# First modulation in two column halves, the first two projection rows in two sets of feature blocks, and the last FFN's sums one pair later

## The chip, the core and the metric

The program runs on one core of a Trainium2 chip. The metric is the time of one execution on the device in microseconds (us); lower is better. The engines are TensorE (PE: matrix multiplies and transposes into PSUM; PEld: its weight loads), VectorE (DVE), ScalarE (ACT), GpSimd (POOL) and SyncE (SP). Here POOL and SP mostly issue DMA transfers, each from its own queue; the transfers of all queues share the core's 16 DMA engines.

## The reference, cut to what matters

Two layers of a diffusion backbone over 1024 latent tokens and 256 context tokens, width D = 1024. Each layer is a mixer and a SwiGLU FFN, each behind a modulated RMS norm. The modulation comes from a conditioning vector, one for the latents and one for the context:

```python
def ada_mod(cond, w, b):
    m = (jax.nn.silu(cond) @ w + b)[..., None, :]
    return jnp.split(m, 6, axis=-1)

def modulate(h, shift, scale):
    return h * (1.0 + scale) + shift
...
        sh1, sc1, g1, sh2, sc2, g2 = ada_mod(c, ada_w[i], ada_b[i])
        u_lat = modulate(rms_norm(h_lat, norm1_g[i]), sh1, sc1)
...
            csh1, csc1, cg1, csh2, csc2, cg2 = ada_mod(c_ctx, ada_w[i], ada_b[i])
            u_ctx = modulate(rms_norm(h_ctx, norm1_g[i]), csh1, csc1)
        if even:
            y_lat = mixer_ab(u_lat, *ab)      # begins with p = u @ w_in, w_in of 1024 x 2048
```

The last FFN is `(silu(u @ w_gate) * (u @ w_up)) @ w_down`, done with Strassen's and Winograd's scheme of seven products on 2 x 2 blocks, which needs sums of blocks of each operand, `w_down` among them.

## The kernel before

Activations lie with features on partitions: u is eight feature blocks of 128 (`KB` = 8), each over three pieces of tokens: pc 0 and pc 1 are 512 latents each, pc 2 the 256 context tokens (`PCS` = (2, 0, 1)). A float32 product is made of three multiplies of rounded parts: each operand is split into hi (`split`: ACT copies with rounding, line 350) and lo (DVE subtracts, line 352), and hi*hi, hi*lo, lo*hi are summed in PSUM by `mm` (line 346).

The head of the program does the following. `filter_mlp` runs a small two-layer MLP with sines (its tail, from line 773, splits the result for the Hyena filters). `ada_first` computes shift and scale of the first norm for both conditions: `ada_pair((1, 0), ...)` loads sixteen tiles `ada_k` of 128 x 1024 (`s<-in_ada_k`, scale and shift for each of eight blocks of the input) through POOL's queue, multiplies them by the two condition columns in four groups of 32 output rows (line 521), copies the rows out, turns them by four transposes (line 536) and adds bias and gain on DVE (lines 543 and 545). `first_norm` loads x and ctx as ten tiles of 128 tokens (`x_row`; tokens 8 and 9 are the context's tiles), squares and scales them by token (lines 698 to 709), and then, for each piece and feature block, transposes (line 727), applies scale and shift while leaving PSUM (DVE line 732, ACT line 734), and splits into u's hi and lo. `in_proj` multiplies output block by output block of w_in ("row" below) against all of u. Its first two rows are done together, three multiplies each per feature block and piece, while `first_norm` is advanced one block at a time by `next(norm)`; the results are copied out at line 1121. The later rows run with other work (filters, spectra, Fourier front) filled in.

A tile scheduler sets the order on each engine from the program and its own estimate of times, within what the data allow; `follow(x)` asks that an instruction be placed behind x. DMA issues are in the order of their queue, POOL's by `ldr`, SP's by `ld`. Pools have a fixed number of buffers: `s4` 21 tiles of 128 x 1024, `ws` 4, `wh` and `wl` 2 each, PSUM six banks `ps` and two `pq`.

In the last FFN (`ffn` with l = 1) eleven pairs of hidden blocks are worked off one after the other; in pair i the helper `sums(k)` (lines 1995 to 2008) loads four quarters of w_down, makes four sums on DVE (2003 to 2006) and stores them for the later `down`; pair i takes k = 2i-2 and 2i-1.

Of the kernel before, what the change touches and what calls it, by code (L numbers as in the profile page):

```python
# [18 lines left out]
P = 128  # L19
D = 1024  # L20
# [238 lines left out]
class Builder:  # L259
# [230 lines left out]
    def ada_first(self):  # L490

        nc, a = self.nc, self.a
        cond = self.C(46)
        nc.gpsimd.memset(cond[:, 16:], 0.0)
        self.ld(cond[:, :16], a["cond"])
        nc.scalar.activation(cond[:, :16], cond[:, :16], AF.Silu)
        self.cond32 = cond
        yield
        yield from self.ada_pair((1, 0), self.S4, self.ldr)

    def ada_pair(self, ms, tile, load):
# [10 lines left out]

        first = ms == (1, 0)
        ps = self.PP()
        ready = fetch(0)
        for kb in range(KB):
# [8 lines left out]
            yield  # L525
        if first:
            self.ada_mm = last
# [4 lines left out]
        if first:  # L532
            self.pk = (self.pk + 1) % self.banks
        for k in range(4):
# [3 lines left out]
        for c in (1, 0):  # L538
            t = self.ada[(0, c)]
            for i, m in enumerate(ms):  # L540
                sl = slice(m * 8, m * 8 + 8)
                two = lambda x: x.rearrange("p (j k) -> p j k", j=2)
                nc.vector.tensor_tensor(two(t[:, sl]), view[:, 2 * i:2 * i + 2, :, c], two(self.adab[:, sl]), ADD)
                if m == 1:
                    nc.vector.scalar_tensor_tensor(t[:, sl], t[:, sl], 1.0, self.gs[:, 0:8], op0=ADD, op1=MUL)
        yield
# [127 lines left out]
    def first_norm(self, u):  # L674
# [5 lines left out]
        for i in groups[0]:  # L680
            rows[i] = self.S4()
            self.ld(rows[i], a["x_row"][i])
        yield
        for i in groups[1]:
# [6 lines left out]
        sq = self.C(10)  # L691

        def scaled(order, cols):
            for k, i in enumerate(order):
                t = self.T(mybir.dt.bfloat16, 1024)
                if k % 2:
                    with self.follow(self.sin):
                        self.sq_act = nc.scalar.activation(t, rows[i], AF.Square, accum_out=sq[:, i:i + 1]).ins
                else:
                    with self.follow(self.clamp):  # L700
                        self.sq_dve = V.tensor_tensor_reduce(t, rows[i], rows[i], 1.0, 0.0, MUL, ADD, sq[:, i:i + 1]).ins
            for c in cols:
                nc.scalar.activation(sq[:, c], sq[:, c], AF.Sqrt, scale=1.0 / D, bias=self.eps)
                V.reciprocal(sq[:, c], sq[:, c])
            for k, i in enumerate(order):
                if k % 2:
                    nc.scalar.mul(rows[i], rows[i], sq[:, i:i + 1])
                else:
                    V.tensor_scalar(rows[i], rows[i], sq[:, i:i + 1], None, op0=MUL)

        scaled(groups[0], (slice(8, 10), slice(0, 4)))
        yield
        for pc in PCS:
            w = WID[pc]
            n = w // P
            if pc == 0:
                scaled(groups[1], (slice(4, 8),))
            u.t.update(self.new_act(pcs=(2,)).t if pc == 2 else {})
            for b in range(KB):
                c0 = b % 2 * w if pc == 2 else 0  # L720
                if c0 == 0:
                    ps = self.PS()
                if pc < 2:
                    u.t.update(self.new_act(pcs=(pc,), blocks=(b,)).t)
                for j in range(n):
                    with self.follow(self.ada_mm):
                        nc.tensor.transpose(ps[:, c0 + j * P:c0 + j * P + P],
                                            rows[OFF.get(pc, LAT) // P + j][:, b * P:b * P + P], self.ident)
                sh, sc = self.ada_col(0, pc, 0, b), self.ada_col(0, pc, 1, b)
                t = self.T()  # L730
                if pc == 2 or b % 2:
                    V.tensor_scalar(t[:, :w], ps[:, c0:c0 + w], sc, sh, op0=MUL, op1=ADD)
                else:
                    nc.scalar.activation(t, ps, AF.Identity, scale=sc, bias=sh)
                self.split(t[:, :w], u.ap(0, b, pc), u.ap(1, b, pc))
                yield

    def filter_mlp(self):
# [12 lines left out]
        for layer, w in enumerate((w1, w2)):  # L751
# [14 lines left out]
            if layer == 0:  # L766
                yield
        self.tap("mlp", x)
# [315 lines left out]

    def in_proj(self, u, norm, fill, four, conv):
        nc, a = self.nc, self.a
# [39 lines left out]
        with self.follow(self.sq_act), self.follow(self.sq_dve):  # L1126
            pairs = [self.weights(a["w_in"][nb]) for nb in (0, 1)]
        p01 = [{}, {}]
        for _ in range(4):
            next(norm)  # L1130
        for pc in PCS:
            accs = [self.PS(), self.PS()]
            for kb in range(KB):
                next(norm, None)
                for r, (wh, wl) in enumerate(pairs):
                    for w, part in ((wh, 0), (wh, 1), (wl, 0)):
                        self.mm(accs[r][:, :WID[pc]], w[:, kb * P:kb * P + P], u.ap(part, kb, pc),
                                kb == 0 and w is wh and part == 0, kb == KB - 1 and w is wl)
            for r in (0, 1):
                p01[r][pc] = kept(r, pc, accs[r])  # L1140
        next(front)
# [846 lines left out]
    def ffn(self, l, u, h, hs, second, after, keep=None, begun={}, early=()):  # L1988
# [59 lines left out]
        for i in range(NFB // 2):  # L2048
# [494 lines left out]
    def run(self):  # L2543
# [23 lines left out]
        next(mlp)  # L2567
        drain(mlp)
        drain(ada1)
        next(ng)  # L2570

# [26 lines left out]
        def conv():  # L2598
# [6 lines left out]
        fc, cc = four(), conv()  # L2605
        self.in_proj(u, ng, ((long, (1, 2, 4, 5, 5, 5, 5, 5, 6, 0)), (filt, (0,) * 9 + (3, 3, 3, 3, 2)),
                             (ada, (0,) * 5 + (1,) * 9)), fc, cc)
# [248 lines left out]
def host_layout(i):  # L2856
# [76 lines left out]
```

## Time and profile before

| | us |
|---|---|
| median of 3 runs (lowest, highest) | 2841.94 (2839.5, 2843.06) |
| profiled execution, its span | 2836.49, 2834.7 |
| TensorE busy over the span | 2756.6 |
| TensorE busy from 0 to 42.4 us, of 42.4 | 22.25 |
| TensorE busy from 42.4 to 81 us, of 38.6 | 36.42 |
| TensorE busy from 2200 to 2560 us, of 360 | 356.03 |

Rows of the timeline begin with the start and the duration, then engine, line, operation, and the tiles written and read by name (`s` is any tile of the s pools, `c` a constant); a bracket gives idle time of that engine just before and what ended it. Rows of groups end with busy time, mean ns of one, and idle time before. In rows of stretches each engine has its busy time and the number of instructions, then come the granted TensorE clock, the busy share of the DMA engines and GB/s. The profiled execution was shorter than all three timed runs, so a sum of its durations has to be set against its own time.

### The profile page before, as it was taken

What the parts mean: (1) busy time and instruction counts of PE and PEld (TensorE: products, weight loads), DVE (VectorE), ACT (ScalarE), POOL (GpSimd) and SP (SyncE); (2) the same over time, 40 slices, a digit from 0 to 9 for tenths busy, and PEclk for the clock granted to TensorE, in tenths of its full rate; (3) what the DMA queues carried; (4) which work ended last, traced back from release to release, by engine and by line L of the source; (5) the groups of instructions that cost most, each with busy time, mean ns of one, the idle gap of its engine ahead of it and who ended that gap; (6) DMA issues with size and microseconds to landing.
All of it is one profiled execution on the core that took longest, in us unless ns stands there. A gap on an engine that the chain in (4) does not pass through costs nothing. (4 is left out here: it accounts for less than half of the span.)

```text
span 2834.7 us, 43636 instructions
## 1 busy us (share of the span) xinstructions
PE 2756.6 (97%) x15610; PEld 2310.1 (81%) x15610; DVE 2042.6 (72%) x3531; ACT 1321.8 (47%) x2271; POOL 552.4 (19%) x896
## 2 busy tenths in 40 slices
PE   6999999999999999999999999999999999999998
PEld 4876778788898888888889888888887788888887
DVE  6777678768877888876777437778868977664555
ACT  5433336443654333343455337878755533333434
POOL 2220335331011222222020002332221122112000
PEclk9999999999999999999999999999999999999999
DMA  7366535665665656658884435877955366435763
GB/s 270 121 193 210 157 93 192 209 220 184 213 207 195 212 198 207 219 204 321 305 306 152 134 115 145 204 199 200 257 192 205 131 240 228 141 104 174 235 193 134
DMA packets 295862, 554.20 MB, mean 196 GB/s; under 512 B 81872, under 2 KB 128658, under 8 KB 295646
## 3 DMA queue, kind: packets, MB, share of 16 engines
q1 hardware_dynamic: 225662, 348.47, 39.6%
q0 software_dynamic: 62784, 189.84, 19.1%
q10 hardware_dynamic: 7200, 13.11, 1.4%
q8 instruction: 123, 2.02, 0.3%
q14 instruction: 93, 0.76, 0.1%
HBM read 405.01 MB, written 118.76 MB: 185 GB/s over the span
## 5 line engine op out<-in xcount | busy, mean ns | idle before, releaser
L1943 PE MATMUL ps<-s,s 128*128 128x512 f32 x2012 | 498.4, 391 | 3.3 <-DVE s L1834 1.7
L1943 PEld LDWEIGHTS ps<-s,s 128*128 128x128 f32 x2012 | 379.2, 189 | 83.9 <-DVE s L1834 2.6
L346 PE MATMUL ps<-s,wh 128*128 128x256 f32 (+1 forms) x1776 | 401.6, 330 | 8.6 <-ACT wh L350 3.8
L346 PEld LDWEIGHTS ps<-s,wh 128*128 128x128 f32 x1776 | 294.2, 189 | 44.2 <-ACT wh L350 5.2
L346 PE MATMUL ps<-s,wl 128*128 128x256 f32 (+1 forms) x888 | 268.1, 328 | 1.5 <-DVE wl L352 1.5
L350 ACT CAST s<-s 128x1024 fp32r<-128x1024 f32 (+2 forms) x196 | 174.9, 921 | 199.6 <-DMA s<-d 178.7
L2120 PE MATMUL ps<-s,s 128*128 128x512 f32 (+1 forms) x1000 | 259.6, 383 | 3.3 <-DVE s L352 3.2
L346 PE MATMUL pq<-s,wh 128*128 128x512 f32 (+1 forms) x848 | 259.7, 388 | 0.8 <-DVE s L2360 0.5
L352 DVE TENSOR_TENSOR wl<-ws,wh 128x1024 fp32r<-128x1024 f32 (+1 forms) x141 | 167.8, 1190 | 121.0 <-ACT wh L350 114.9
L350 ACT CAST wh<-ws 128x1024 fp32r<-128x1024 f32 (+1 forms) x141 | 144.7, 1026 | 211.4 <-PE ps L346 93.2
L352 DVE TENSOR_TENSOR s<-s,s 128x1024 fp32r<-128x1024 f32 (+2 forms) x174 | 193.5, 1143 | 58.1 <-ACT s L350 56.2
L346 PE MATMUL ps<-s,s 128*128 128x65 f16 (+4 forms) x2736 | 224.8, 234 | 2.6 <-DVE s L2479 0.8
L2120 PEld LDWEIGHTS ps<-s,s 128*128 128x128 f32 x1000 | 184.6, 188 | 41.0 <-DVE s L352 4.5
L350 ACT CAST s<-t 128x512 fp32r<-128x512 f32 (+2 forms) x234 | 131.5, 581 | 172.9 <-PE ps L1943 71.8
L352 DVE TENSOR_TENSOR s<-t,s 128x512 fp32r<-128x512 f32 (+2 forms) x234 | 148.1, 647 | 74.7 <-ACT s L350 54.0
L1943 PE MATMUL ps<-s,wh 128*128 128x512 f32 x624 | 194.8, 390 | 0.0
L337 POOL DMA_DIRECT2D d<-s x202 | 110.0, 546 | 379.1 <-DVE s L1750 90.5
L346 PEld LDWEIGHTS ps<-s,wl 128*128 128x128 f32 x888 | 164.5, 189 | 19.3 <-DVE wl L352 2.1
L346 PEld LDWEIGHTS pq<-s,wh 128*128 128x128 f32 x848 | 150.2, 189 | 23.0 <-DVE c L871 0.8
L346 PE MATMUL pq<-s,wl 128*128 128x512 f32 (+1 forms) x424 | 161.5, 381 | 0.7 <-DVE wl L352 0.7
L2120 PE MATMUL ps<-s 128*128 128x512 f32 (+1 forms) x500 | 150.7, 385 | 0.0
L346 PEld LDWEIGHTS ps<-s,s 128*128 128x128 f32 (+1 forms) x816 | 126.2, 191 | 20.2 <-issue 2.0
(489 smaller groups left out, 5460.3 us busy)
## 6 DMA issues: line engine op xcount, KB each, us to landing
s<-d SPq DMA_DIRECT2D x282, 256.0 KB, 4.1
d<-s POOLq DMA_DIRECT2D x186, 256.0 KB, 3.7
s<-in_down SPq DMA_DIRECT2D x150, 256.0 KB, 4.6
s<-in_ada_w POOLq DMA_DIRECT2D x64, 512.0 KB, 5.0
ws<-in_up SPq DMA_DIRECT2D x44, 512.0 KB, 3.8
d<-g POOLq DMA_DIRECT2D x86, 256.0 KB, 3.1
ws<-in_gate SPq DMA_DIRECT2D x42, 512.0 KB, 5.3
d<-tk POOLq DMA_DIRECT2D x66, 256.0 KB, 4.0
```

Of the source, the lines that this page charges most:

```text
L337: self.last_ldr = self.nc.gpsimd.dma_start(out, in_).ins
L346: self.last_mm = self.nc.tensor.matmul(o, l, r, start=st, stop=sp).ins
L350: self.last_hi = nc.scalar.copy(hi, src).ins
L352: self.last_lo = eng.tensor_tensor(lo, src, hi.bitcast(F32), SUB).ins
L1943: nc.tensor.matmul(ps, x[:, sl], y, start=first and j == 0 and x is wh and y is xh, stop=j == 3 and x is wl, skip_group_check=True)
L2120: m = nc.tensor.matmul(acc[j][:, c0:c1], x[:, sl], y[:, xs], start=first and k == 0, stop=last and k == 2, skip_group_check=True)
```

## The change

1. The weights of the first modulation are laid out anew (`ada_h`): half j holds the columns 512j to 512j+511 of scale and shift, that is, what feature blocks 4j to 4j+3 need, in eight tiles. `ada_half(0)` runs before the projection; `ada_half(1)` is loaded behind it and multiplied tile by tile inside the first two rows.
2. The two rows run in four steps (`STEPS`): context blocks 0 to 3, first latents (pc 0) blocks 0 to 7, context blocks 4 to 7, second latents (pc 1). The sums of all pieces stay in PSUM until their step is done.
3. The two rows' weights are loaded on POOL's queue between the halves, each in two column pieces, and split in two pieces. The squares and scalings of the rows of x are spread over the steps, and the MLP's tail is moved to the eighteenth of the 24 block steps.
4. In the last FFN pair i takes the sums k = 2i-4 and 2i-3.

```diff
+STEPS = ((2, range(4)), (0, range(KB)), (2, range(4, KB)), (1, range(KB)))
...
-        yield from self.ada_pair((1, 0), self.S4, self.ldr)
+        yield from self.ada_half(0)
+
+    def ada_half(self, j):
...
+        for kb in range(KB):
+            ws.append(self.S4())
+            self.ldr(ws[-1], a["ada_h"][j, kb])
+        yield
+        ps = self.PP()
+        for kb in range(KB):
+            with self.follow(self.last_mm if j else None):
+                for g in range(4):
+                    self.ada_mm = nc.tensor.matmul(ps[32 * g:32 * g + 32, :256], cond[:, 2 * kb:2 * kb + 32],
+                                                   ws[kb][:, g * 256:(g + 1) * 256], start=kb == 0, stop=kb == KB - 1,
+                                                   tile_position=(0, 32 * g), skip_group_check=True).ins
+            yield
+        row = self.G()
+        nc.vector.tensor_copy(row[:, :256], ps[:, :256])
+        col = self.PP()
+        last = self.ada_mm
+        for k in (0, 1):
+            with self.follow(last):
+                self.col_tr = nc.tensor.transpose(col[:, k * P:(k + 1) * P], row[:, k * P:(k + 1) * P], self.ident).ins
...
     def first_norm(self, u):
...
+        for i in (8, 9, 0, 1):
+            square(i, self.sin1, self.clamp if i == 0 else self.clamp1)
+        root(slice(8, 10), self.sin)
+        for i in (8, 9):
+            scale(i)
+        for i in (2, 3):
+            square(i, self.sc_act, self.clamp)
+        yield
...
-        for pc in PCS:
+        first = self.ada_mm
+        for pc, kbs in STEPS:
...
+            if (pc, kbs[0]) == (0, 0):
+                with self.follow(self.last_hi), self.follow(self.last_lo):
+                    for i in groups[0][2:]:
+                        scale(i)
...
+                if (pc, b) == (0, 5):
+                    for i in groups[1][:2]:
+                        square(i, self.last_hi, self.last_lo)
...
     def in_proj(self, u, norm, half, mlp, first_w, fill, four, conv):
...
+        def first_split(c, act, dve):
+            for t, (hi, lo) in zip(first_w, pairs):
+                with self.follow(act), self.follow(dve):
+                    self.split(t[:, c], hi[:, c], lo[:, c])
...
+        for pc, kbs in STEPS:
+            if kbs[0] == 0:
+                sums[pc] = [self.PQ() if pc == 2 else self.PP() for _ in (0, 1)]
+            for kb in kbs:
...
+                        with self.follow(self.col_tr if n == 6 else None):
+                            self.mm(sums[pc][r][:, :WID[pc]], w[:, kb * P:kb * P + P], u.ap(part, kb, pc),
+                                    kb == 0 and w is wh and part == 0, kb == KB - 1 and w is wl)
+                if n < 5:
+                    for _ in range(1 + n // 2 - n // 4):
+                        next(half)
...
+                if n == 3:
+                    first_split(slice(512, D), self.last_hi, self.last_lo)
+                if n == 17:
+                    with self.follow(self.last_hi), self.follow(self.last_lo):
+                        for _ in mlp:
+                            pass
...
     def ffn(self, l, u, h, hs, second, after, keep=None, begun={}, early=()):
-            for k in (2 * i - 2, 2 * i - 1) if l == 1 else (9, 10) if i == 9 else (i,) if i < 9 else ():
+            for k in (2 * i - 4, 2 * i - 3) if l == 1 else (9, 10) if i == 9 else (i,) if i < 9 else ():
...
     def run(self):
+        for _ in range(9):
+            next(ada1)
+        first_w = [self.W("ws", "ws") for _ in (0, 1)]
+        for c in (slice(0, 512), slice(512, D)):
+            for nb, t in enumerate(first_w):
+                with self.follow(self.last_ldr):
+                    self.ldr(t[:, c], a["w_in"][nb][:, c])
+        half = self.ada_half(1)
...
+    o["ada_h"] = f["ada_w"][0, :, :2 * D].reshape(KB, P, 2, 2, 512)[:, :, ::-1].transpose(3, 0, 1, 2, 4).reshape(2, KB, P, D)
```

The order that results, at three places. Line numbers of the kernel after are higher by one (helpers), by 59 (`first_norm`) or by 87 (`ffn`).

First, POOL's queue in the head. Before, the end of the sixteen modulation tiles and what follows (`ws` is a staging buffer of w_in; w_in 0 and 1 went through SP's queue):

```order
L337 DMA s_65_232<-in_ada_k 128x1024
L337 DMA s_66_234<-in_ada_k 128x1024
L337 DMA s_69_254<-in_x_row 128x1024
L337 DMA s_70_256<-in_x_row 128x1024
L337 DMA s_71_258<-in_x_row 128x1024
L337 DMA s_72_260<-in_x_row 128x1024
L337 DMA s_73_262<-in_sgn 128x512
L337 DMA ws_747<-in_w_in 128x1024
```

Now, from the seventh tile of half 0:

```order
L338 DMA s_56_188<-in_ada_h 128x1024
L338 DMA s_57_190<-in_ada_h 128x1024
L338 DMA ws_225<-in_w_in 128x512
L338 DMA ws_226<-in_w_in 128x512
L338 DMA ws_225<-in_w_in 128x512
L338 DMA ws_226<-in_w_in 128x512
L338 DMA s_61_231<-in_ada_h 128x1024
```

The first two rows of w_in stand behind eight modulation tiles, and the other eight tiles, the four rows of x and all else behind them.

Second, TensorE from the modulation to the first projection multiplies (L536 and L525 turn the modulation's rows, L727 and L786 are transposes of rows of x, s_28 and s_29 the context's, s_30 to s_33 latents'; wh and wl are w_in's parts). Before:

```order
L521 MATMUL ps_175<-s_66_234,c_102 32x512 x2
L727 MATMUL pq_322<-c_86,s_28_117 128x128
L727 MATMUL pq_322<-c_86,s_29_119 128x128
L727 MATMUL pq_430<-c_86,s_30_121 128x128
L727 MATMUL pq_430<-c_86,s_31_123 128x128
L727 MATMUL pq_430<-c_86,s_32_125 128x128
L727 MATMUL pq_430<-c_86,s_33_127 128x128
L536 MATMUL ps_243<-c_86,g_240 128x128 x2
```

Now, the same place behind half 0:

```order
L515 MATMUL ps_192<-s_57_190,c_102 32x256 x4
L525 MATMUL ps_259<-c_86,g_257 128x128 x2
L786 MATMUL ps_297<-c_86,s_28_117 128x128
L786 MATMUL ps_297<-c_86,s_29_119 128x128
L786 MATMUL ps_314<-c_86,s_28_117 128x128
L786 MATMUL ps_314<-c_86,s_29_119 128x128
L786 MATMUL ps_297<-c_86,s_28_117 128x128
L786 MATMUL ps_297<-c_86,s_29_119 128x128
L347 MATMUL pq_327<-s_108_289,wh_283 128x256
```

and, further on, the end of half 1 (s_65 to s_68 are its last four tiles):

```order
L515 MATMUL ps_349<-s_65_239,c_102 32x256 x4
L515 MATMUL ps_349<-s_66_241,c_102 32x256 x4
L347 MATMUL ps_426<-s_125_334,wh_283 128x512
L347 MATMUL ps_427<-s_125_334,wh_285 128x512
L347 MATMUL ps_426<-s_125_334,wh_283 128x512
L347 MATMUL ps_426<-s_125_334,wl_284 128x512
L347 MATMUL ps_427<-s_125_334,wh_285 128x512
L347 MATMUL ps_427<-s_125_334,wl_286 128x512
L515 MATMUL ps_349<-s_67_243,c_102 32x256 x4
L515 MATMUL ps_349<-s_68_245,c_102 32x256 x4
```

The multiplies of half 1 stand among those of the projection: all context blocks 0 to 3 and latent block 0 before its last two tiles.

Third, DVE in the last FFN where the first sums stood (L2003 to L2006 are the sums, L1967 leaves PSUM, L2042 ends pair 0). Before:

```order
L352 TENSOR_TENSOR wl_24446<-ws_24441,wh_24445 128x1024
L2003 TENSOR_TENSOR s_5286_24338<-s_5285_24337,s_5286_24338 128x512
L1929 TENSOR_TENSOR t_24386<-ws_24369,t_24374 128x512
L2042 TENSOR_TENSOR tk_24086<-g_24071,tk_24057 128x512
L1967 TENSOR_TENSOR g_24262<-pq_24223,g_24262 128x512
L2004 TENSOR_TENSOR s_5285_24337<-s_5287_24339,s_5285_24337 128x512
L2003 TENSOR_TENSOR s_5290_24354<-s_5289_24353,s_5290_24354 128x512
```

Now:

```order
L353 TENSOR_TENSOR wl_24461<-ws_24456,wh_24460 128x1024
L2016 TENSOR_TENSOR t_24401<-ws_24384,t_24389 128x512
L353 TENSOR_TENSOR s_5293_24393<-t_24389,s_5292_24392 128x512
L2129 TENSOR_TENSOR tk_24133<-g_24118,tk_24104 128x512
L353 TENSOR_TENSOR s_5295_24397<-t_24388,s_5294_24396 128x512
L353 TENSOR_TENSOR s_5299_24404<-t_24400,s_5298_24403 128x512
L2054 TENSOR_TENSOR g_24309<-pq_24270,g_24309 128x512
```

Between the same neighbours now stand splits of the pair's weight sums (L353) in place of the sums of w_down.

More of the change, by code (lines that the diff above doesn't have):

```diff
@@ L525, in ada_pair @@
             yield
-        if first:
-            self.ada_mm = last
         row = self.G()
@@ L690, in first_norm @@
             self.ldr(self.sgn, a["sgn"][:, :512])
[L691 to L709, printed above, removed]
@@ L1083, in short_conv, with in_proj @@
         return z
-    def in_proj(self, u, norm, fill, four, conv):
+    def in_proj(self, u, norm, half, mlp, first_w, fill, four, conv):
         nc, a = self.nc, self.a
@@ L1124, in kept @@
             return t
-        with self.follow(self.sq_act), self.follow(self.sq_dve):
-            pairs = [self.weights(a["w_in"][nb]) for nb in (0, 1)]
+        pairs = [self.pair2() for _ in (0, 1)]
+        def first_split(c, act, dve):
+            for t, (hi, lo) in zip(first_w, pairs):
+                with self.follow(act), self.follow(dve):
+                    self.split(t[:, c], hi[:, c], lo[:, c])
         p01 = [{}, {}]
-        for _ in range(4):
+        for k in range(4):
             next(norm)
[L1131 to L1134, printed above, removed]
+            if k == 0:
+                first_split(slice(0, 512), self.sq_act, self.last_ev)
@@ L1139, in in_proj @@
-            for r in (0, 1):
-                p01[r][pc] = kept(r, pc, accs[r])
+                        with self.follow(self.col_tr if n == 6 else None):
[4 more added lines that the diff above has]
+                        next(half)
+                if n == 4:
+                    next(half)
+                    next(norm)
+                    next(norm)
@@ L1141, in in_proj @@
+                if n == 3:
+                    first_split(slice(512, D), self.last_hi, self.last_lo)
+                if n == 17:
+                    with self.follow(self.last_hi), self.follow(self.last_lo):
+                        for _ in mlp:
+                            pass
+                n += 1
+            if kbs[-1] == KB - 1:
+                for r in (0, 1):
+                    p01[r][pc] = kept(r, pc, sums[pc][r])
+        self.pk = (self.pk + 4) % self.banks
         next(front)
@@ L2567, in run @@
         next(mlp)
-        drain(mlp)
+        next(mlp)
+        next(ng)
+        for _ in range(9):
[6 more added lines that the diff above has]
+        half = self.ada_half(1)
+        next(half)
+        next(ng)
         drain(ada1)
-        next(ng)
         def filters():
```

73 lines of the change are left out of this document (56 added, 17 removed).

## The prediction

> **What bounds the kernel now.** I read the page first, for the busy shares and the 40 slices.
>
> ```profile
> span 2834.7 us, 43636 instructions
> PE 2756.6 (97%) x15610; PEld 2310.1 (81%) x15610; DVE 2042.6 (72%) x3531; ACT 1321.8 (47%) x2271; POOL 552.4 (19%) x896
> PE   6999999999999999999999999999999999999998
> ```
>
> TensorE (PE) is busy 97% of the span. Of its 78 idle us the largest share lies in the first slice, the only one with a 6. The change rewrites just that slice, and one detail of the last FFN. So I read the busy time by stretches of the head (columns: PE, weight load, DVE, ACT, POOL busy, granted clock, DMA share, GB/s), and then TensorE's timeline there.
>
> ```profile
> 14.00:24.00 10.00, 7.10 (x35) 1.61 (x34) 8.58 (x14) 2.89 (x6) 2.14 (x5) 1.00 1.03 418
> 24.00:38.00 14.00, 8.70 (x35) 1.23 (x34) 6.38 (x11) 8.46 (x13) 4.55 (x9) 1.00 1.03 419
> 42.40:81.00 38.60, 36.42 (x212) 30.79 (x212) 26.46 (x46) 24.11 (x43) 1.59 (x3) 1.00 0.25 81
> ```
>
> ```profile
> 15.12 4.15 PE L521 MATMUL ps<-s,c 128*32 128x512 f32 x24
> 23.22 1.05 PE L521 MATMUL ps<-s,c 128*32 128x512 f32 x4 [1.47 <-DMA s<-in_ada_k]
> 33.51 1.05 PE L521 MATMUL ps<-s,c 128*32 128x512 f32 x4 [0.21 <-DMA s<-in_ada_k]
> 34.76 1.05 PE L521 MATMUL ps<-s,c 128*32 128x512 f32 x4 [0.20 <-DMA s<-in_ada_k]
> 36.94 1.05 PE L521 MATMUL ps<-s,c 128*32 128x512 f32 x4 [1.12 <-DMA s<-in_ada_k]
> 42.39 0.50 PE L346 MATMUL ps<-s,wh 128*128 128x256 f32 x2
> 80.56 0.39 PE L346 MATMUL ps<-s,wl 128*128 128x512 f32 x1
> 81.40 1.44 PE L346 MATMUL ps<-s,wh 128*128 128x256 f32 x6 [0.46 <-ACT wh L350]
> ```
>
> Until 38 us the DMA engines are full (share 1.03, 418 GB/s) and TensorE multiplies the modulation's weights tile by tile as they land (L521, four instructions a tile, sixteen tiles, each wait ending on DMA in_ada_k). The last starts at 36.94. The modulation must be complete before any block of u can be scaled, so the first projection multiply comes at 42.39, 4.4 us after the last modulation multiply ends (36.94 + 1.05 = 37.99). From there the stage is TensorE's: 36.42 busy of 38.60 us, and the first two projection rows end at 80.56 + 0.39 = 80.95. The next row begins at 81.40 and TensorE is then nearly full. So what counts is how much earlier than 80.95 these two rows end.
>
> **Part 1: modulation in two column halves, weights earlier.** The bytes stay the same: sixteen 512 KB tiles, and w_in 0 and 1. The order changes: eight tiles of half 0, w_in in four pieces, then the eight tiles of half 1. The POOL queue and the SP queue (six rows of x) shared the engines; the queues' rows are
>
> ```profile
> 25.17 0.53 POOL L337 DMA_DIRECT2D s<-in_x_row  x1 [0.92 <-DMA s<-in_ada_k]
> 11.37 22.79 SPq L331 DMA_DIRECT2D ws<-in_w_in  x4
> 29.01 1.04 ACT L350 CAST wh<-ws 128x1024 fp32r<-128x1024 f32 x1 [3.94 <-DMA ws<-in_w_in]
> ```
>
> The tiles counted on TensorE (six in the x24, then one per row) make the row at 23.22 the eighth. Half 0's eighth tile lands in the same place of the same queue, so half 0 ends its multiplies at 23.22 + 1.05 = 24.3 instead of 38.0. In the last column of the POOL row the first x_row, seventeenth in the queue, waits for an in_ada_k to land just behind the eighth: as I read it a transfer goes out when one eight places ahead has landed, so I expect no gap behind half 0. A tile alone takes 34.76 - 33.51 = 1.25 us: w_in lands by about 25.8 (before, its first cast waited till 29.01), half 1 by 25.8 + 8 x 1.25 = 35.8, about the 36.9 of before.
>
> What follows half 0 is a chain on DVE, ACT and TensorE.
>
> ```profile
> L543 DVE TENSOR_TENSOR c<-ps,c 128x8 f32<-128x8 f32 x4 | 0.4, 159 | 0.7 <-PE ps L536 0.7
> L732 DVE TENSOR_SCALAR t<-ps,c 128x256 f32<-128x256 f32 x6 | 3.1, 540 | 0.5 <-PE ps L727 0.5
> L352 DVE TENSOR_TENSOR s<-t,s 128x256 fp32r<-128x256 f32 x8 | 3.4, 422 | 0.2
> L350 ACT CAST s<-t 128x256 fp32r<-128x256 f32 x8 | 3.2, 404 | 5.7 <-DVE t L732 5.6
> L350 ACT CAST s<-t 128x512 fp32r<-128x512 f32 x16 | 9.3, 624 | 4.3 <-DVE t L732 4.2
> L352 DVE TENSOR_TENSOR s<-t,s 128x512 fp32r<-128x512 f32 x16 | 10.5, 686 | 5.7 <-ACT s L350 5.6
> L734 ACT ACTIVATE t<-ps,c 128x512 f32<-128x512 f32 x5 | 3.9, 780 | 0.0
> L709 DVE TENSOR_SCALAR s<-s,c 128x1024 f32<-128x1024 f32 x2 | 1.4, 750 | 0.0
> L707 ACT ACTIVATE s<-s,c 128x1024 f32<-128x1024 f32 x2 | 2.2, 1156 | 0.0
> ```
>
> By these durations: four adds 0.4 to 1.1 with their wait, eviction 0.54, cast 0.40, and for the copy, two transposes and two scalings ahead of and between them I estimate 1 us: the first projection multiply 3 us after 24.3, at 27.3. By the 4.4 us that the same chain took before it would be 28.7, and later if the two w_in subtractions now queued ahead (2 x 0.69 on DVE) hold it up: 30.1. I take 27.7, near the sum of durations, because the rows that it needs (tokens of the context, 8 and 9) are scaled beforehand. The context's blocks 0 to 3 then run at DVE's pace (0.54 + 0.42 less overlap, about 0.8 us a block), to about 31.5.
>
> **Part 2: what TensorE still has to do.** Its work from 27.7 on: the 36.42 us of the stretch above, some six transposes that lay ahead of 42.4 (0.6), half 1's eight tiles and its two transposes (0.4). A tile cost 4.15 / 6 = 0.69 us back to back and 1.05 alone. Half the columns mean twice the instructions for the same streamed columns, so the eight cost 5.5 to 8.4 us; I take 5.5, since they now stand between other TensorE work. Before, such multiplies filled idle time; now they are on the path, which is the price of the change. Idle time: 38.60 - 36.42 = 2.2 us before; bounds 0.5 and 6, since ACT and DVE get more between the blocks (two squares, two scalings of 0.75 and 1.16 us, w_in's second halves, and the filter MLP's casts, all now inside the stage); I take 2.2. End: 27.7 + 36.4 + 0.6 + 5.5 + 0.4 + 2.2 = 72.8, so 80.95 - 72.8 = 8.15 us earlier. Best ends together: 27.3 + 37.4 + 5.5 + 0.5 = 70.7, gain 10.3; a further 1 to 3 us if half 1 falls into TensorE's waits at 31 to 36. Worst ends: 30.1 + 37.4 + 8.4 + 6 = 81.9, loss 1.
>
> The moved waits: in TensorE's queue half 1's multiplies stand ahead of the latent blocks 0 and 1, so a late half 1 holds these up; it lands by 36 and the blocks' operands (row scaling 1.16, eviction 0.78, cast 0.62, subtraction 0.69 each behind 31.5) are ready only at 36. On ACT two squares now stand ahead of the MLP's second sine, which nothing needs before the seventeenth step. On the POOL queue the last four rows of x move behind half 1 as they did, and the next two w_in rows behind them: they are needed at the stage's end, some 30 us later, so they cost nothing; without that cover each would be 1.25. SP's queue loses the first two w_in transfers of its row above. After the two rows everything follows in the same order, relative to their end, and TensorE stays the bound; I carry the whole gain through.
>
> **Part 3: the last FFN's sums a pair later.**
>
> ```profile
> 2252.66 3.02 PE L1943 MATMUL pq<-s,s 128*128 128x512 f32 x12 [0.68 <-ACT g L1948]
> 2257.32 0.69 DVE L2003 TENSOR_TENSOR s<-s,s 128x512 f32<-128x512 f32 x1 [2.61 <-DMA s<-in_down]
> 2260.00:2280.00 20.00, 20.00 (x89) 16.54 (x89) 18.88 (x31) 8.34 (x14) 3.98 (x9) 1.00 0.73 260
> 2500.00:2520.00 20.00, 20.00 (x90) 16.57 (x89) 11.46 (x17) 7.86 (x13) 1.62 (x3) 1.00 0.30 105
> ```
>
> Where the first sums stand, DVE waits 2.61 us for their loads, but TensorE loses only 0.68 us; later it is full. The move can gain 0 to 0.7 us; the sums end in pair 7 instead of 5, where DVE has room (11.46 of 20). I take 0.7.
>
> **Sum.** 8.15 + 0.7 = 8.85 us. The profiled execution took 2836.49 us (span 2834.7 and 1.8 around it), 5.45 below the median 2841.94 of the runs; on it the sum gives 2827.6, on the median 2833.1, which is what I predict. A measurement of this kernel tells about 0.2% (5.7 us) from no change.
>
> **Rivals.**
>
> First, the clock. Rows that bear on it:
>
> ```profile
> 13.71 0.33 PEld L346 LDWEIGHTS ps<-s,t 128*128 128x128 f32 x1 [0.52 <-issue]
> 44.06 0.28 PE L346 MATMUL ps<-s,wh 128*128 128x256 f32 x1
> 44.18 0.28 PE L346 MATMUL ps<-s,wl 128*128 128x256 f32 x1
> 37.92 0.31 PEld L727 LDWEIGHTS pq<-c,s 128*128 128x128 f32 x3 [0.84 <-issue]
> 2210.00:2214.00 4.00, 1.01 (x4) 0.44 (x3) 4.00 (x7) 3.25 (x6) 0.00 (x0) 0.81 0.00 0
> 2214.00:2218.00 4.00, 4.00 (x10) 3.13 (x11) 4.00 (x7) 2.16 (x4) 0.00 (x0) 0.50 0.00 0
> ```
>
> One 128x128 weight load took 0.33 us at 13.7, and three took 0.31 together at 37.9: TensorE had sped up during the modulation's multiplies. At 2210 it was busy 1.01 of 4 us, and the granted clock then fell to 0.50. Now 24.3 to 27.7 holds only eight transposes. If the clock halves there, the 24 context multiplies (44.18 - 44.06 = 0.12 us apart) and some 16 transposes take 4 us more; DVE's pace covers about 1: 3 us less gain, 2836.1. The Trainium skill (TensorE: Matmul & The Clock Gate, Part 1) says that a window of about 3.4 us without activity halves the clock, and sustained work restores it. By that rule, with the stretch of 3.4 us just at the edge, the halving would come or not by where the window lies; the trace's fall at 2210 agrees. Against it: the gaps of up to 1.5 us between tiles never showed it. Chance 0.14.
>
> Second, the stage waits instead of working: half 1's rows late on the queue, or latent blocks held up by ACT. With 6 us idle and tiles at 8.4 the gain is 1 to 2 us plus 0.7: 2839.5. For it: from 42.4 to 81 ACT and DVE had 24 and 26 of 38.6 us, and get about 6 more each. Against: both still have room, and that half 0 should not come first is excluded by POOL's order. Chance 0.13.
>
> Third, the cheap case: half 1 fills the waits, gain 11 to 13, 2830. Chance 0.17.
>
> Fourth, slower: the last FFN. TensorE's order in its pairs 1 and 2 is rewritten, and a wait as at 2210 costs 3 us idle and 2.6 at low clock, 5.6. Two such waits cancel the gain, three give 2841.94 - 8.15 + 16.8 = 2850.6. Against: TensorE had 20.00 of 20 there with the sums ahead. Chance 0.06.
>
> **Chances.** My forecast has 0.50, with a range of its own of 2830.5 to 2836.5. Faster: 0.47 of it, 0.17, 0.08 of the clock case: 0.72. Same: the rest of the clock case, the second rival, 0.03: 0.22. Slower: 0.06. Range 2827 to 2839.5: it leaves out the slower rival, half of the second and a tail of the third.
>
> **What would show it.** In the profile after: the first L347 multiply at about 27.7 and half 1's last L515 near 39; w_in's cast not waiting for DMA; the row that follows the two at about 73 instead of 81.4; TensorE busy over 90% from 32 to 73; the stages behind shifted by the same 8 us; no 0.68 wait at the first sums. Wrong, if L515 stands in line behind a DMA after 38, if the clock reads 0.50 before 40, or if the gain at 73 is gone by 200.

## The result, and the profile after

The changed kernel took 2826.92 us (median of 6 runs, 2825.13 to 2830.19), the kernel before 2841.06 us (6 runs, 2837.16 to 2847.05). The ratio is 0.995 with a 95% interval of 0.9937 to 0.9962: 14.1 us faster, by the interval 10.8 to 17.9. The forecast was 2833.1 us, with 2827.0 as the low end of its range. So the direction was right, and the gain was 5 us larger than the sum of 8.85 us.

The page after, against the lines shown of before (its profiled execution took 2830.19 us, the slowest of the six):

```profile
span 2828.1 us, 43782 instructions
PE 2757.1 (97%) x15674; PEld 2317.3 (82%) x15674; DVE 2045.2 (72%) x3540; ACT 1323.1 (47%) x2272; POOL 556.4 (20%) x900
PE   7999999999999999999999999999999999999998
```

TensorE's first slice went from 6 to 7; its busy time is the same within 1 us although it issues 64 more instructions. Its timeline in the head (L515 modulation, L525 its transposes, L347 projection):

```profile
23.30 1.08 PE L515 MATMUL ps<-s,c 128*32 128x256 f32 x8 [1.80 <-DMA s<-in_ada_h]
25.02 0.66 PE L525 MATMUL ps<-c,g 128*128 128x128 f32 x2 [0.64 <-DVE g L520]
27.46 1.52 PE L347 MATMUL pq<-s,wh 128*128 128x256 f32 x3
40.68 1.07 PE L515 MATMUL ps<-s,c 128*32 128x256 f32 x16
72.14 0.39 PE L347 MATMUL ps<-s,wl 128*128 128x512 f32 x1
72.99 0.39 PE L347 MATMUL ps<-s,wh 128*128 128x256 f32 x1 [0.46 <-ACT wh L351]
```

Half 0 ends at 24.38, the first projection multiply comes at 27.46 (forecast 27.7), half 1's last tiles follow other work without a wait, the two rows end at 72.53 (forecast 72.8), and the next row begins at 72.99, where the profile of before had 81.40. By stretches (columns as before; the third number from the end is the granted clock):

```profile
22.50:32.60 10.10, 8.18 (x37) 6.33 (x38) 8.55 (x24) 7.14 (x14) 4.88 (x9) 0.50 1.03 410
33.00:72.60 39.60, 39.44 (x262) 29.91 (x260) 26.87 (x52) 25.46 (x47) 4.78 (x9) 1.00 0.51 183
```

The clock stood at 0.50 from 22.4 to 32.7 us, the event of the first rival. Behind it TensorE is busy 39.44 of 39.60 us. So the new head is where the sum had put it, 8.4 us earlier than in the one profile of before, and the head explains 8.4 of 14.1. The question of the experiments was where the other 5 to 6 us are.

### The profile page after: what moved, and what is told of

It is laid out like the page before. It is cut to its first block, busy times and chain, and to the rows that moved or that the text cites. A ratio compares the mean times of both kernels' runs of the same rounds, so it can differ in the third digit from the quotient of the medians.

```text
span 2828.1 us, 43782 instructions
## 1 busy us (share of the span) xinstructions
PE 2757.1 (97%) x15674; PEld 2317.3 (82%) x15674; DVE 2045.2 (72%) x3540; ACT 1323.1 (47%) x2272; POOL 556.4 (20%) x900
## 5 line engine op out<-in xcount | busy, mean ns | idle before, releaser
L347 PE MATMUL ps<-s,wh 128*128 128x256 f32 (+1 forms) x1744 | 397.4, 332 | 7.2 <-ACT wh L351 3.8
L347 PEld LDWEIGHTS ps<-s,wh 128*128 128x128 f32 x1744 | 290.0, 189 | 43.3 <-ACT wh L351 5.3
L347 PE MATMUL pq<-s,wh 128*128 128x512 f32 (+1 forms) x880 | 268.8, 387 | 0.5 <-ACT wh L351 0.3
L347 PE MATMUL ps<-s,wl 128*128 128x256 f32 (+1 forms) x872 | 263.6, 330 | 1.5 <-DVE wl L353 1.5
L351 ACT CAST wh<-ws 128x1024 fp32r<-128x1024 f32 (+2 forms) x143 | 145.2, 1017 | 224.6 <-PE ps L347 100.0
L353 DVE TENSOR_TENSOR wl<-ws,wh 128x1024 fp32r<-128x1024 f32 (+2 forms) x143 | 168.7, 1182 | 111.2 <-ACT wh L351 105.2
L353 DVE TENSOR_TENSOR s<-s,s 128x1024 fp32r<-128x1024 f32 (+2 forms) x174 | 193.7, 1145 | 56.4 <-ACT s L351 53.7
L347 PE MATMUL ps<-s,s 128*128 128x65 f16 (+4 forms) x2736 | 225.3, 234 | 2.8 <-DVE s L2566 1.1
L353 DVE TENSOR_TENSOR s<-t,s 128x512 fp32r<-128x512 f32 (+2 forms) x234 | 148.6, 650 | 75.5 <-ACT s L351 45.9
L347 PEld LDWEIGHTS ps<-s,wl 128*128 128x128 f32 x872 | 162.5, 190 | 19.4 <-DVE wl L353 2.1
L347 PEld LDWEIGHTS pq<-s,wh 128*128 128x128 f32 x880 | 157.3, 191 | 22.7 <-ACT wh L351 0.7
L347 PE MATMUL pq<-s,wl 128*128 128x512 f32 (+1 forms) x440 | 166.7, 379 | 0.8 <-DVE wl L353 0.8
L347 PEld LDWEIGHTS ps<-s,s 128*128 128x128 f32 (+1 forms) x816 | 126.2, 192 | 21.3 <-PE ps L347 2.3
```

What stands on the lines that cost most here:

```text
L347: self.last_mm = self.nc.tensor.matmul(o, l, r, start=st, stop=sp).ins
L351: self.last_hi = nc.scalar.copy(hi, src).ins
L353: self.last_lo = eng.tensor_tensor(lo, src, hi.bitcast(F32), SUB).ins
```

## The experiments

**Both parts alone.** Three theories: A, the sum holds and single executions differ; B, the sums of the last FFN are worth about 5 us; C, the head's gain grows behind 73 us. Four kernels were timed beside the kernel before (2838.93 us, 23 runs).

The changed kernel again, no edit:

> The changed kernel once more, for a second profile and more times. The first profile of it shows the row behind the first two starting 8.4 us earlier (72.99 instead of 81.40) and the span only 6.6 us shorter, while the medians of six runs each stand 14.1 us apart (2826.92 and 2841.06). Theory A (the sum of the prediction, 8.85 us, holds; the rest is how single executions differ): the ratio of this measurement lands near 2832/2841 = 0.997, and two executions of one kernel differ in their profiles by some us outside the rewritten places. Theory B (the last FFN's sums are worth about 5 us in most executions, not 0.7) and theory C (the head's gain grows behind the row at 73 us): 14 us again, ratio 0.995. In all of them the row behind the first two starts at 73.0 within 0.5 us.

Measured: 2826.08 us, ratio 0.9957 (0.9944 to 0.9969), so 12.2 us faster (8.8 to 15.9). The row behind the first two began at 73.01.

The head alone:

```
-  for k in (2 * i - 4, 2 * i - 3) if l == 1 ...
+  for k in (2 * i - 2, 2 * i - 1) if l == 1 ...
```

> The changed kernel with the last FFN's sums put back to pairs 2i-2 and 2i-1; the head as changed. Theory A: 8.2 us under the kernel before (ratio 0.9971) and 0.7 us over the changed kernel. Theory B: 8.4 to 9 us under before, about 5 us over the changed kernel. Theory C: 13 us under before (ratio 0.9953), within 1 us of the changed kernel.

Measured: 2828.15 us, ratio 0.9966 (0.9954 to 0.9977): 9.7 us (6.5 to 13.1).

The sums alone, the opposite edit in the kernel before:

> The kernel before with only the last FFN's sums moved to pairs 2i-4 and 2i-3. Theory A: 0.7 us under the kernel before, not to be told from it. Theory B: about 5 us under (ratio 0.9982). Theory C: as A. In the profile the wait of 0.68 us of TensorE at the first sums (at 2252 us) is gone in all of them.

Measured: 2835.76 us, ratio 0.9993 (0.9981 to 1.0005): 2.0 us, from 5.4 faster to 1.4 slower.

The kernel before, unchanged:

> The kernel before itself, unchanged, against itself: it shows how far two measurements of one kernel can differ, and gives a second profile of it. All theories: ratio 1.000 within 0.001. Theory A expects its profile to differ from the first in a few stretches by 2 to 4 us in both directions (the stretches where the granted clock read 0.50 for 3.4 us, nine of them in the first profile of before, and the stretch from 770 to 870 us, where multiplies of 256 columns came 113.3 ns apart before and 117.8 ns after). Theories B and C expect the profiled execution of before (2836.49 us) to have been an exception, and this one's span near 2839.

Measured: 2838.98 us, ratio 1.0005 (0.9996 to 1.0013). Its span was 2836.1.

The middle values, some 10 us for the head and some 2 for the sums, speak against B's 5 us and C's 13 us. Alone they do not settle it: the intervals reach 5.4 for the sums and 13.1 for the head, and they hold the forecast's 0.7 and 8.15 as well. The profiles below settle B and C (the sums change their stretch by 1 to 3 us, and the head's gain grows by about 1 us behind 73). The new profiles of before also showed what the sum had overlooked. Here the one of the unchanged kernel; TensorE's first and last row of the stage have L346 now as in the first profile:

```profile
43.10 0.80 PE L346 MATMUL ps<-s,wh 128*128 128x256 f32 x2
84.78 1.44 PE L346 MATMUL ps<-s,wh 128*128 128x256 f32 x6 [0.46 <-ACT wh L350]
```

The row that began at 81.40 in the execution from which the forecast was read begins at 84.78 here, and at 84.72 in the kernel with the sums alone, whose head is that of before. In both the granted clock was 0.50 for about 10 us between 25 and 60 us. In the first profile it was 1.00 throughout the head. This gives theory D: the base was a lucky execution, lucky in just the stage that the change rewrites.

**How often is the head of before disturbed?** Three more profiles of the unchanged kernel before, and one of the changed one, each a single execution.

> The kernel before, unchanged: a profile alone, to see how often its head runs at half clock. Of four profiles so far (this kernel twice, once with the sums moved, which leaves the head alone, and once with idle multiplies that fill the waits) the two without filled waits after the first showed the granted clock at 0.50 for about 10 us between 25 and 60 us and the row behind the first two at 84.8; the one that the prediction was read from showed neither, row at 81.4. Theory D (the prediction's base was the rare case): 0.50 within the first 60 us and the row at 84 to 85.5. Theory E (a rare accident on the other side): full clock, row at 81.4.

> The same once more. Theory D: 0.50 in the head and the row at 84 to 85.5 in most of the three. Theory E: in none, or one.

> The same once more. Theory D: 0.50 in the head and the row at 84 to 85.5 in most of the three. Theory E: in none, or one.

> The changed kernel, unchanged, a profile alone. All theories: the clock at 0.50 from 22.4 to 32.7 us and the row behind the first two at 73.0 to 73.3, as in its other profiles; the stretch of 256-column multiplies near 770 to 860 us at 113.3 ns a multiply, as in seven of eight profiles (117.8 in the first profile of the changed kernel), or, if that second pace is as frequent as the first, again 117.8.

Their times were 2833.3, 2835.1 and 2835.89 us, and 2824.57 us for the changed kernel. In the first of the three TensorE begins the projection when it did in the first profile (42.37 against 42.39), and only the clock differs; these are TensorE's rows and the stretch:

```profile
42.37 0.80 PE L346 MATMUL ps<-s,wh 128*128 128x256 f32 x2
84.36 1.44 PE L346 MATMUL ps<-s,wh 128*128 128x256 f32 x6 [0.46 <-ACT wh L350]
```

```profile
42.40:60.00 17.60, 15.48 (x93) 14.27 (x94) 15.28 (x30) 12.66 (x25) 1.60 (x3) 0.81 0.50 162
```

So the clock alone cost 3.0 us there. In the second the clock was full, and the start was late:

```profile
32.47 1.04 ACT L350 CAST wh<-ws 128x1024 fp32r<-128x1024 f32 x1 [1.46 <-DMA ws<-in_w_in]
```

```profile
43.36 0.51 PE L346 MATMUL ps<-s,wh 128*128 128x256 f32 x2
82.38 1.43 PE L346 MATMUL ps<-s,wh 128*128 128x256 f32 x6 [0.46 <-ACT wh L350]
```

```profile
42.40:60.00 17.60, 14.95 (x105) 13.16 (x106) 16.32 (x32) 13.64 (x27) 1.60 (x3) 1.00 0.53 173
```

The second w_in row landed a microsecond later than in the first profile, where its cast reads

```profile
31.50 1.05 ACT L350 CAST wh<-ws 128x1024 fp32r<-128x1024 f32 x1 [1.45 <-DMA ws<-in_w_in]
```

and ACT, in order, scaled the rows of x that much later (its three scalings start at 37.16 instead of 36.20). All heads together, each line one execution:

| head | first projection multiply | clock 0.50 within the first 60 us | next row |
|---|---|---|---|
| before, first profile | 42.39 | never | 81.40 |
| before, fourth profile | 43.36 | never | 82.38 |
| before, fifth profile | 42.68 | 22.7 to 26.1, 53.5 to 56.9 | 82.85 |
| before, third profile | 42.37 | 25.2 to 28.6, 42.2 to 45.6, 55.9 to 59.3 | 84.36 |
| before, sums alone | 43.76 | 30.8 to 34.2, 41.0 to 47.9 | 84.72 |
| before, second profile (again) | 43.10 | 25.3 to 28.7, 42.3 to 45.7, 56.0 to 59.4 | 84.78 |
| after, five profiles | 27.29 to 27.65 | 22 to 33, each | 72.80 to 73.30 |

The mean of the six is 83.4, of the five 73.0 (72.99, 73.01, 72.80; head alone 73.30; the last kernel below 73.13). So the head gains 10.4 us on the average and 8.4 on the luckiest base. In four of the six the clock fell, and none began the projection earlier than the first profile by more than 0.02 us. As a whole the first execution was not that lucky: at 2836.49 us it was longer than the third to fifth (2833.3 to 2835.89), although their heads ended later. So its luck lay in the head, and the time of the whole execution did not show it.

**Taking the clock away as a cause.** Idle multiplies in the places where TensorE waits for tiles, in the kernel before:

```
 for i in (0, 1):
     ... four multiplies of the tile
+    if ms == (1, 0) and 2 * kb + i in (6, 7, 9, 10, 11):
+        for j in (0, 1, 1):
+            ...
+            matmul(ps[g:g + 30, :], cond[:, 16:46], ws[i][...], start=False, stop=False)   # zero weights
 ...
+ ... four more behind the modulation's transposes
```

> The kernel before, with 19 idle TensorE multiplies added in the head (weights that are zero, so that they add nothing): three behind each of five modulation tiles, where TensorE waited for the next tile, and four behind the modulation's transposes; no other engine's order changes. Theory D (the profiled execution of before that the prediction was read from had the head at full clock, while most executions of before have the granted clock at 0.50 for 3.4 to 10 us there, as the second and third profile of it show: the row behind the first two starts at 84.8 in both, not at 81.4): no 0.50 before 60 us, that row at 81.4 to 82, and the median 2 to 3.4 us under the kernel before (ratio 0.9988 to 0.9993). Theory E (the later row has another cause, and the surplus lies elsewhere): the row stays at 84 to 85, ratio 1.000.

Measured: 2840.93 us, ratio 1.0004 (0.9994 to 1.0015). The profile, by stretch and at the next row:

```profile
24.00:42.40 18.40, 15.94 (x80) 4.36 (x76) 7.91 (x19) 10.23 (x15) 5.43 (x11) 1.00 1.03 417
42.40:60.00 17.60, 15.35 (x109) 13.32 (x106) 16.31 (x32) 13.84 (x28) 1.60 (x3) 1.00 0.53 173
```

```profile
82.20 1.43 PE L346 MATMUL ps<-s,wh 128*128 128x256 f32 x6 [0.46 <-ACT wh L350]
```

The clock stayed at 1.00 and the row came at 82.20, 1.2 us under the mean of the six, but the time did not follow: theory D's 2 to 3.4 us are not there. The interval still holds 1.2 us. So the disturbed heads are shown in profiles; that they make up the surplus of the medians is not shown by this run.

The same in the changed kernel, behind the last three tiles of half 0 (the added multiplies write beside half 0's sums and alter the modulation's values, not the work):

```
+ for _ in range({5: 1, 6: 2, 7: 1}.get(kb, 0) if j == 0 else 0):
+     for g in range(4):
+         matmul(ps[32 * g:32 * g + 32, 256:], cond[...], ws[kb][...], start=True, stop=True)
```

> The changed kernel, with 16 idle TensorE multiplies (their result is not read) behind the last three tiles of half 0, where TensorE waits 1.9 us twice and the granted clock then reads 0.50 from 22.4 to 32.7 us in all three profiles of it. Theory D: the clock stays at 1.00 in the head, the 24 context multiplies come 0.12 us apart instead of 0.21, and the row behind the first two starts 1.5 to 2.6 us earlier (70.4 to 71.5 instead of 73.0); the median 1 to 2.6 us under the changed kernel. Theory E or a rival that DVE sets the pace of the context blocks anyway: the row at 72.5 to 73, the same time as the changed kernel.

Measured: 2825.35 us, ratio 0.9945 (0.993 to 0.9961), not to be told from the changed kernel. The stretch shown above for the changed kernel, and TensorE's rows:

```profile
22.50:32.60 10.10, 6.71 (x56) 4.77 (x52) 8.03 (x24) 6.85 (x13) 4.37 (x8) 1.00 1.03 406
```

```profile
28.95 0.38 PE L347 MATMUL pq<-s,wh 128*128 128x256 f32 x1 [1.05 <-DVE s L353]
73.23 1.43 PE L347 MATMUL ps<-s,wh 128*128 128x256 f32 x6 [0.46 <-ACT wh L351]
```

The clock is full, and the row comes at 73.23, no earlier. At full clock TensorE waits for DVE's splits instead (1.05 us at 28.95, and more idle elsewhere: 6.71 busy of 10.10 against 8.18). ACT's scaling of the first latent rows, which the latent blocks need, starts at the same time at half clock, in the changed kernel,

```profile
30.98 2.19 ACT L733 ACTIVATE s<-s,c 128x1024 f32<-128x1024 f32 x2
```

and at full clock, here:

```profile
31.08 2.19 ACT L738 ACTIVATE s<-s,c 128x1024 f32<-128x1024 f32 x2
```

So in the new order the clock's fall lies beside the pace of DVE and ACT. The first rival happened, and its price was about 0, not 3 us.

**What the overlap is worth.** All of half 1 ahead of the projection:

```
  p01 = [{}, {}]
+ for _ in half:
+     pass
  ...
```

> The changed kernel with all eight tiles of half 1 multiplied, and their transposes and sums issued, ahead of the first projection block, as the whole modulation stood before the change; the loads stay in the changed order. By the prediction's account (half 1 costs 5.5 us of TensorE time on the path but lets the projection begin ten us earlier): half 1's last tile at 37 to 38, the first projection multiply at 40 to 41, TensorE's 37.4 us of work and 1 to 2 us idle behind it, the row behind the first two at 78.5 to 81 instead of 73.0: 5.5 to 8 us slower than the changed kernel. A rival (the earlier loads of w_in and the rows scaled beforehand brought most of the gain): the row at 76 or earlier, under 3 us slower than the changed kernel.

Measured: 2837.47 us, ratio 0.9982 (0.9972 to 0.9993): 5 us under the kernel before (2 to 8, the moved sums among them), and by the ratios some 7 to 9 us over the changed kernel. TensorE's rows:

```profile
35.20 3.53 PE L515 MATMUL ps<-s,c 128*32 128x256 f32 x24 [1.86 <-DMA s<-in_ada_h]
41.53 0.80 PE L347 MATMUL pq<-s,wh 128*128 128x256 f32 x2
81.88 1.43 PE L347 MATMUL ps<-s,wh 128*128 128x256 f32 x6 [0.46 <-ACT wh L351]
```

The row is back at 81.88. The earlier loads of w_in and the rows scaled beforehand bring little by themselves, 1.5 us against the mean of the six (83.4) and nothing against the first profile (81.40); most of the head's gain is that the projection begins while half 1 is still landing. (The row is a microsecond beyond the expected range. The clock read 0.50 from 24.5 to 31.3 and from 34.7 to 44.9 us; that this made the microsecond is not shown.)

**The sums.** I matched the instructions of each profile with those of the first and took how much longer or shorter the stretch from 2245 to 2350 us is (on the first profile's scale). With the sums of before: 0.0 in the first profile, then 0.44, 0.10, 0.73 and 0.90 in the second to fifth, with idle multiplies 1.68, with the head alone 2.22. With the sums moved, in every profile, -0.98. The waits of TensorE and of DVE there, in the kernel with the head alone:

```profile
PE ps L2030 <- DVE g L2054: 1.3, 1, 1.3
PE pq L2030 <- ACT g L2035: 0.7, 1, 0.7
```

```profile
DVE s L2090 <- DMA s<-in_down: 6.5, 2, 3.5
DVE s L2093 <- DMA s<-in_down: 3.9, 1, 3.9
DVE s L2091 <- DMA s<-in_down: 0.4, 1, 0.4
```

and of DVE in the third profile of the changed kernel, in which TensorE waits for nothing between 2240 and 2300:

```profile
DVE s L2091 <- DMA s<-in_down: 4.5, 2, 3.0
DVE s L2090 <- DMA s<-in_down: 2.0, 1, 2.0
```

DVE's wait for w_down's tiles summed to 7 to 11 us in the old place, and in the new place it is there too (6.5 us in these rows); what differs is whether it reaches TensorE. Beyond the 0.68 that the forecast priced, a wait for DVE's evictions (L2054) appears on TensorE in some executions with the sums in the old place, by up to 1.3 us. TensorE's waits do not make up all of the spread: up to some 0.8 us of a longer stretch stands in no wait of the rows. Is there more to take? One pair later still:

```
-  for k in (2 * i - 4, 2 * i - 3) if l == 1 ...
+  for k in (2 * i - 6, 2 * i - 5) if l == 1 ...
```

> The changed kernel with the last FFN's sums one pair later still (2i-6 and 2i-5). In the six profiles with the sums of the kernel before, the stretch from 2245 to 2350 us took 0.0 to 2.2 us longer than in the first profile; in the six with the sums moved it took 0.98 us less than there, the same to 0.01 us. Theory S1 (the move took away a wait for w_down's loads that reached TensorE in a different measure in each execution, and nothing is left to take): the same stretch again at 0.98 us less, no wait of TensorE for the pairs' evictions there, and the time that of the changed kernel (ratio to before 0.9945 to 0.9965). Theory S2 (DVE's work in the early pairs is what costs, so that each pair of delay gains): a further 1 us less there, and the ratio below 0.9950. A loss of 1 us or more near 2350 to 2500 would speak for neither: then the sums come too late for their readers.

Measured: 2822.68 us against 2836.94 of before, ratio 0.9951 (0.9937 to 0.9966); the stretch is 0.98 us shorter again. S1 holds: TensorE's wait is gone, and nothing is left there. The interval of the ratio reaches into the ranges of both theories; the stretch decides. The mean of the seven old stretches is 0.87, so the move is worth 1.8 us (1.0 to 3.2 against single profiles, not B's 5).

## Why the prediction was right or wrong

**The head after: right.** The first multiply at 27.46 (27.7), the end at 72.53 (72.8), 45.07 us between them (45.1 forecast). w_in's casts no longer wait for DMA, TensorE was above 90% from 33 on. Two terms under the sum were off and met: TensorE idled 0.2 us, not 2.2, and was busy 44.8 us, not 42.9, because the half clock until 32.7 stretched its work; with the clock full it waited instead and ended no earlier. Half 1's last tile ended at 41.75, not near 39.

**The step that failed: the base.** "It gives 2827.6 on the profiled execution, on the median 2833.1." The sum was measured from 80.95, the end of the two rows in one execution that was 5.45 us under the median, and the same microseconds were put on the median. That holds only if what made this execution fast lies outside the change. About 2.9 of the 5.45 us lay inside: the next row began earliest of six (2.0 under the mean), and the stretch of the sums was the shortest of seven (0.87 under the mean). In the changed places the executions of before differ: w_in lands earlier or later on SP's queue, the clock falls or not, a wait for DVE reaches TensorE or not. In the five profiles with the changed head the next row lies within 0.5 us, so the gain is larger against the usual execution than against the best. 10.4 + 1.8 = 12.2 us, within both intervals (10.8 to 17.9; 8.8 to 15.9), against 8.85, which the first interval leaves out and the second just holds. The sum on the profiled execution, 2827.6, came within 1 us of the measured time; as only part of that execution's lead lay in the changed places, some of this is luck.

**Part 3: mis-sized.** 0.7 was the one wait on TensorE that the base showed; it measured 0.98 on that base and 1.8 on the mean. (The kernel's code ends the sums in pair 6 before and in pair 7 now, counted from 0; the prediction's 5 was a slip that its sum does not use.)

**The first rival: it happened, at no cost.** I had named a clock of 0.50 before 40 us as a sign against the forecast; it came, and the row stood at 73. It came earlier than the rival had it: at 22.4, behind waits for half 0's last tiles (TensorE busy 0.64 us of the 3.4 before), not in the stretch of transposes from 24.3. And I asked only whether the clock would fall in the kernel after, and not whether it falls in the kernel before, where it did in four of six heads and cost up to 3 us. What I held against it, that gaps of up to 1.5 us between tiles never showed it, held for one execution: in the second and third profile the clock fell at 25.3 and 25.2 behind such gaps (1.46 and 1.44 us). The first profile of before had full clock until 215 us and hid it. The second rival (idle 6 us) and the fourth (a loss in the last FFN) did not come; of the third, the nearly full TensorE came (idle 0.2 us), but not a further gain.

**Carrying through.** The mean span of the five profiles of the unchanged kernel before is 2833.9 us, of the three of the changed kernel 2824.1: 9.8 us, less than the 12.2 of the two places and than the 12.2 and 14.1 of the timed runs. Between 200 and 640 us single executions gain or lose up to 5 us against the first profile, in both kernels, mostly in stretches in which the clock falls in one and not in the other; so a few profiles cannot tell 9 from 13: the first pair differed by 6.6 us of span, the medians by 14.1.

**Open.** The timed surplus over 12.2 us, some 0 to 2 us, and whether the medians' surplus over 8.85 us comes from the two places at all: the profiles show it there, the times are too coarse to confirm it. Behind 140 us the changed kernels gain about 1 us more by 205 us (their offset grows by 0.5 to 0.8 there, that of before by 0.3 the other way on the mean); I have no run that names its cause. And the filled kernel before should have shown part of the clock's cost in its time, and did not. The time of before itself moved between 2836.94 and 2841.25 us from one set of runs to the next, so the forecast of a gain can be judged better than that of a time.

## What to carry to other kernels

A profile is one execution. Before a sum is made against it, ask whether the stage to be changed is where it was lucky. The time of the whole execution does not answer that: three later profiles of before were shorter as a whole and had longer heads. More profiles of the kernel before answer it, read at that stage; two or three would have shown the row at 82 to 85 and cost less than any experiment here. A change that takes away a wait of variable length should be priced with the mean of the wait, not with the value in the trace at hand.

## What the runs showed of the hardware

The granted clock fell in units of 3.413 us (3.4, 6.8, 10.2) on a grid of its own, which does not start with the program (the first falls in the head of before come at 22.7, 25.2, 25.3 and 30.8 us; in the five profiles with the changed head, at 22.2 to 23.3, they lie closer). Laid on that grid, over all fourteen profiles, 108 windows at full clock were followed by one at half (the fall at the program's end left out): 58 of them had TensorE busy under 45% of the window, 44 between 45 and 61%, 6 above 80%. Only three windows under 45% were not followed by a fall, the lowest at 43%; between 45 and 61%, some 70 were not. So a fall does not need an idle window: under 45% it nearly always came, up to 61% it came or not. What decides there, and what made the six falls above 80%, these traces do not show. The Trainium skill (TensorE: Matmul & The Clock Gate, Part 1) says that the window is free-running and 3413 ns long; these traces agree. It gives an idle window as the condition; here the measurement decides: tiles that keep TensorE busy for 1.05 us in every 2.5 were enough in two heads of before (the falls at 25.2 and 25.3).

A stretch of 256-column multiplies that waits for nothing ran at two paces. TensorE from 800 to 820 us, in the first profile of the changed kernel and then in its second:

```profile
800.00:820.00 20.00, 20.00 (x172) 20.00 (x171) 14.65 (x18) 10.73 (x16) 1.63 (x3) 1.00 0.64 207
```

```profile
800.00:820.00 20.00, 20.00 (x179) 20.00 (x178) 14.44 (x19) 10.68 (x16) 2.16 (x4) 1.00 0.67 219
```

172 multiplies against 179, 117.8 ns apart against 113.3, both at full clock with the weight load (PEld) busy throughout. The stretch lasts from 760 to 870 us, and the slower pace cost some 4 us. It came in one of the fourteen profiles, the first of the changed kernel; without these 4 us that execution would lie among its others. I do not know what sets it.
